# One PSUM bank set from o-projection to down, pools for the next stage's first weights, token sums ahead, and the final norm in halves

## The chip, the cores and the metric

The kernel runs on one core of a Trainium2 chip. The metric is device time in microseconds (us) of one execution. TensorE multiplies matrices into PSUM, eight banks of 512 float32 columns on 128 partitions. VectorE (DVE in the rows), ScalarE (ACT) and GpSimd (POOL) do the element-wise work; SyncE (SP) and ScalarE's queue issue the DMAs. Each engine works through its own queue in order.

## What is computed

The reference is one layer of a hybrid trunk on 2048 frames of a prompt and 8 × 16 frames of running streams, 17 tiles of 128 tokens with 1024 channels. All is float32.

```python
h = rmsnorm(x, norm_mix_pre)
P = h @ w_in
...
o, S_new = gated_delta_rule(q, k, v, g, beta, S0, chunk)
...
mix = jnp.concatenate([o, sc_out.astype(x.dtype)], axis=-1) @ w_o
x = x + rmsnorm(mix, norm_mix_post)

h = rmsnorm(x, norm_ffn_pre)
f = (jax.nn.silu(h @ w_gate) * (h @ w_up)) @ w_down
x = x + rmsnorm(f, norm_ffn_post)
```

`w_gate` and `w_up` are 1024 × 2816, `w_down` is 2816 × 1024.

## The kernel before

A product of two float32 matrices is made of three: each operand is split into a high part, a cast to the multiplier's format, and a low part, the difference. So each weight or token tile needs a cast, on ScalarE, and a subtraction, on VectorE or POOL. Gate/up and down add a seven-product scheme on 2 × 2 blocks in place of eight products, which needs sums of blocks on both sides before the split.

The stages follow each other:

1. In-projection and the gated delta rule, to about 1027 us. The change leaves it alone.
2. o-projection, one `o_tile(t)` (L695) per tile, 17 of them: load `mr` (one buffer) and `xo`, split `mr` in two halves into `mh`, `ml` (L705, L706, three buffers each), 48 matmuls (L711), squares of the sums (L715), norm and addition to `xo` (L720, L721), store to `x2d` (L722), squares of `xo` (L724), scaling of `xo` in place (L727), 8 transposes (L733), scaling by a gain into `ht` (L734), store to `hTd` (L737). After 14 tiles, `ffn_prep(0, ...)` makes the token parts of the first group.
3. Gate/up in three groups of 6, 6 and 5 tiles (`FGROUPS`), 22 blocks f of weights in each. `gate_up` (L903) makes seven products for an f: A11, S3, S1, S2, A12, A22, S4, of 12 matmuls each (L900), 84 in all, with 384 columns (320 in the last group). `gu_weights` loads `rg` and `ru`, makes the sums `sA` to `sD` (L868 to L871) and the seven `fw` pairs (cast L878, subtraction L879), in a ring of 12 pairs. This is done in group 0 only; the pairs with sums are stored in `fsplit` and loaded again in groups 1 and 2. `ffetch` fetches the weights of one f ahead. What comes out of the banks is combined (L918 to L935) into `pt`, seven parts per pair of f (L946 to L956), which goes to `partd` (L958).
4. Between groups, `ffn_prep` makes 28 token parts of the next group: 7 names (B11, T3, T1, T2, B21, T4, B22) for 4 k. Each needs a cast into `xh` (L835) and a subtraction into `xl` (L836); T3, T1, T2, T4 need a block difference first (L821 to L830). The tokens `fh` of the next group are loaded at the start of the group before.
5. Down, five chunks of f (`FCHUNKS`: 4, 4, 4, 4, 6 blocks), in each 8 pairs of token tiles and a single one. `down_pair` (L1051) loads parts `ar`, splits them into `as` (L1011, L1012), and makes seven products (L1028); the last chunk has 63 matmuls per pair. The weight pairs `dw` (L770, L772) live in a ring of 22, 3 of them in an early pool; `prep_step` makes them, some ahead of the next chunk by `spare`. Bank sums are added to `acc` on VectorE (L986).
6. In the last chunk `finish` (L1031) makes the last norm of a tile: load `xr`, square, `rstd` (a step on VectorE, L126, then a power on POOL, L128), multiplication by the gain `gpo` (L1039, on POOL but for the last pair), one operation for scale and addition (L1040), store.

Each stage takes its eight banks from a pool of its own: `psd`, `pst`, `pft` for the o-projection, `psf` for gate/up, `psy` for down. A pool's memory becomes free when the pool before it is closed. Within this, a scheduler that simulates the engines sets the order of the instructions in each queue. `V`, `G`, `A`, `T` are VectorE, POOL, ScalarE and TensorE.

## Time and profile before

| | us |
|---|---|
| runs of the kernel before | 2707.65, 2709.2, 2717.58 |
| median | 2709.2 |
| the profiled execution | 2705.94 |
| its span in the profile | 2704.2 |
| TensorE busy in the span | 2542.4 |
| VectorE, POOL, ScalarE busy | 1687.6, 949.5, 948.0 |

The views are read like this. A row of the timeline gives start, duration, engine, line, operation, output and input, the count, and in brackets how long the engine had stood idle and what ended it. The table of windows gives, for each stretch, the busy time and the count of each engine and the granted clock of TensorE (1.00 is full). L numbers are lines of the kernel before.

### The profile page before, as it was taken

The page shows a single profiled execution, that of the slowest core. Times are in us where ns is not written, and L with a number is a line of the kernel's source. Part 1 is how long each engine was busy: PE and PEld are TensorE (multiplying, and loading weights), DVE is VectorE, ACT ScalarE, POOL GpSimd, SP SyncE. Part 2 cuts the span into 40 slices and gives each one's busy share as a digit, 9 for nine tenths or more (in the row PEclk, how much of TensorE's full clock was granted, in tenths as well). Part 3 has the DMA queues.
Part 4 walks back from the last instruction along what each step waited for, and adds up shares of the span by engine and source line. Part 5 has one row for each costly group of instructions (what it writes and reads, how often), then busy time and mean ns, then how long its engine had stood idle before and what let it go on. Part 6 is the DMA issues. An engine that isn't in the chain of part 4 may idle for free.

```text
span 2704.2 us, 41766 instructions
## 1 busy us (share of the span) xinstructions
PE 2542.4 (94%) x15105; PEld 2359.3 (87%) x15105; DVE 1687.6 (62%) x3341; ACT 948.0 (35%) x2256; POOL 949.5 (35%) x845
## 2 busy tenths in 40 slices
...
PEclk9889999999999999998999989999999989999999
...
GB/s 304 291 306 257 221 212 197 232 195 209 221 215 208 186 237 136 241 167 237 283 259 268 259 223 275 242 257 240 231 310 280 270 176 96 123 121 122 134 203 167
DMA packets 314270, 595.70 MB, mean 220 GB/s; under 512 B 55260, under 2 KB 204704, under 8 KB 292560
## 3 DMA queue, kind: packets, MB, share of 16 engines
...
HBM read 434.04 MB, written 158.90 MB: 219 GB/s over the span
## 4 chain that ended last, share of the span: by engine, by line
PE 39%; DVE 9%; issue 3%; DMA 3%; POOL 2%; ACT 1%; ACTq 1%; SPq 0%; POOLq 0%; DVEq 0%
PE fbank L900 28%; PE ybank L1028 10%; DMA mr<-mixd 1%; DVE xl L836 1%; DMA dr<-in_w_dn 1%; DVE xr L1040 1%; DVE acc L986 1%; POOL as L1012 1%; DMA ru<-in_w_gu 1%; ACTq L958 0%; DVE as L1012 0%; DMA x2d<-xo 0%; POOL dw L772 0%; DVE fw L879 0%; POOL f2r L128 0%
## 5 line engine op out<-in xcount | busy, mean ns | idle before, releaser
L900 PE MATMUL fbank<-xh,fw 128*128 128x384 f32 (+1 forms) x3696 | 906.8, 329 | 17.6 <-ACT m L918 7.4
L134 PE MATMUL dbank<-hi,w 128*128 128x384 f32 (+1 forms) x2688 | 704.0, 341 | 35.3 <-ACT w L293 11.8
L900 PEld LDWEIGHTS fbank<-xh,fw 128*128 128x128 f32 x3696 | 657.4, 190 | 23.8 <-ACT m L918 8.5
L900 PE MATMUL fbank<-xl,fw 128*128 128x384 f32 (+1 forms) x1848 | 605.4, 328 | 2.7 <-DVE xl L836 2.5
L134 PEld LDWEIGHTS dbank<-hi,w 128*128 128x128 f32 x2688 | 493.0, 196 | 48.2 <-ACT w L293 13.6
L1028 PE MATMUL ybank<-dw,as 128*128 128x512 f32 x1980 | 462.5, 395 | 23.7 <-DVE acc L986 10.9
L1028 PEld LDWEIGHTS ybank<-dw,as 128*128 128x128 f32 x1980 | 373.6, 190 | 112.4 <-issue 9.9
L134 PE MATMUL dbank<-lo,w 128*128 128x384 f32 (+1 forms) x1344 | 453.3, 337 | 0.0
L900 PEld LDWEIGHTS fbank<-xl,fw 128*128 128x128 f32 x1848 | 350.0, 190 | 3.2 <-DVE xl L836 2.8
L134 PEld LDWEIGHTS dbank<-lo,w 128*128 128x128 f32 x1344 | 263.9, 196 | 2.2 <-issue 0.2
L879 POOL TENSOR_TENSOR fw<-rg,fw 128x512 fp32r<-128x512 f32 x132 | 184.6, 1399 | 180.6 <-ACT fw L878 180.6
L1012 POOL TENSOR_TENSOR as<-ar,as 128x256 fp32r<-128x256 f32 (+1 forms) x200 | 181.1, 915 | 138.3 <-ACT as L1011 134.6
L986 DVE TENSOR_TENSOR acc<-acc,ybank 128x512 f32<-128x512 f32 x248 | 166.8, 683 | 98.9 <-PE ybank L1028 83.3
L1011 ACT CAST as<-ar 128x256 fp32r<-128x256 f32 (+1 forms) x290 | 118.6, 427 | 196.0 <-PE ybank L1028 135.1
L505 POOL MEMSET AU<- 32x128 f32 x16 | 3.1, 195 | 409.1 <-PE gbank L491 383.7
L878 ACT CAST fw<-rg 128x512 fp32r<-128x512 f32 x132 | 82.4, 624 | 152.2 <-PE fbank L900 137.0
L879 POOL TENSOR_TENSOR fw<-ru,fw 128x512 fp32r<-128x512 f32 x66 | 97.0, 1469 | 108.2 <-ACT fw L878 95.2
L320 DVE SCALAR_TENSOR_TENSOR acc<-R,cw,acc 128x384 f32<-128x384 f32 (+1 forms) x216 | 129.9, 605 | 1.6
L927 DVE TENSOR_TENSOR u<-m,fbank 128x384 f32<-128x384 f32 (+1 forms) x66 | 34.8, 528 | 152.8 <-PE fbank L900 147.8
L928 POOL TENSOR_TENSOR m<-m,m 128x384 f32<-128x384 f32 (+1 forms) x66 | 70.2, 1064 | 148.4 <-ACT m L920 114.2
L932 DVE TENSOR_TENSOR c<-u,fbank 128x384 f32<-128x384 f32 (+1 forms) x66 | 34.9, 528 | 127.7 <-PE fbank L900 127.6
L772 POOL TENSOR_TENSOR dw<-dr,dw 128x512 fp32r<-128x512 f32 x52 | 75.5, 1465 | 29.1 <-ACT dw L770 29.0
...
## 6 DMA issues: line engine op xcount, KB each, us to landing
...
```

The source lines that it names most:

```text
L134: T.matmul(ps, l, r, start=(i == 0), stop=(i == n - 1))
L320: V.scalar_tensor_tensor(acc, raw(d), w[:, d:d + 1], acc, op0=ALU.mult, op1=ALU.add)
L772: e.tensor_tensor(out=w[:, 1], in0=v, in1=w[:, 0].bitcast(F32), op=ALU.subtract)
L878: A.copy(w[:, 0], v)
L879: e.tensor_tensor(out=w[:, 1], in0=v, in1=w[:, 0].bitcast(F32), op=ALU.subtract)
L900: T.matmul(ps, w_[:, c], b_[k][:, :hw], start=(first and k == 0 and ci == 0), stop=(k == KH - 1 and ci == 2), skip_group_check=not first)
L928: G.tensor_tensor(out=s7, in0=s7, in1=s5, op=ALU.add)
L932: V.tensor_add(c21, u2, b3)
L986: V.tensor_add(dst, dst, ps)
L1011: A.copy(a[:, 0, :n], v)
L1012: e.tensor_tensor(out=a[:, 1, :n], in0=v, in1=a[:, 0, :n].bitcast(F32), op=ALU.subtract)
L1028: T.matmul(ps, a[:, x_, q * P:(q + 1) * P], w[:, y_], start=(start and q == 0 and ci == 0), stop=(q == c - 1 and ci == 2), skip_group_chec ...
```

## The change

- **Banks.** `psd`, `pst` and `pft` stay open to the end; `fbank()` goes round their 8 banks in gate/up and down. `psf` and `psy` are gone.
- **o-projection.** `xo` is scaled into a new tile `hx`; `mh` and `ml` have 2 buffers instead of 3; `wor` shares the buffers of `xo`.
- **First weights of gate/up.** A pool `fe` holds `rg`, `ru`, the sums and 3 of the 12 `fw` pairs. It opens ahead of the last three o tiles; `gu_weights` is now a generator, and its first 3 pairs are asked for before the last o tile, the other 4 after it. The subtraction of S4 is on POOL instead of VectorE.
- **Token sums ahead.** `ffn_sums` makes T3 (in 4 buffers) and T1 of the next group inside the group before, all on VectorE. In `ffn_prep` VectorE has 12 of the `xl` subtractions and POOL 16 (14 and 14 before, and POOL had two of the T3).
- **pt and a21** have one buffer instead of two.
- **Down.** 4 instead of 3 weight pairs in the early pool, the ring is 21 instead of 22; the seven parts of the first pair are loaded into a tile `ar0` when the early pool opens, in group 2 at f = 10.
- **Final norm.** Squares, products and additions in halves of 512 columns; the multiplication by `gpo` is one VectorE operation with the scale (none on POOL), the addition another; the halves are stored by ScalarE's and SP's queues. In the last chunk the split of the fourth part is on POOL.

Cut to its core:

```diff
...
-NDR = 3
-NDW = 22
+NDR = 4
+NWE = 3
+NDW = 21
...
-            wr = op.tile([P, D], F32, tag="wor", name="wor", bufs=2)
+            wr = op.tile([P, D], F32, tag="xo", name="wor", bufs=2)
...
-                mh = op.tile([P, KD // 2, P], F32R, tag="mh", name="mh", bufs=3)
-                ml = op.tile([P, KD // 2, P], F32R, tag="ml", name="ml", bufs=3)
+                mh = op.tile([P, KD // 2, P], F32R, tag="mh", name="mh", bufs=2)
+                ml = op.tile([P, KD // 2, P], F32R, tag="ml", name="ml", bufs=2)
...
-            V.tensor_scalar_mul(xt, xt, r)
+            hx = op.tile([P, D], F32, tag="hx", name="hx")
+            V.tensor_scalar_mul(hx, xt, r)
...
+    def fbank():
+        i = nbank[0] % 8
+        nbank[0] += 1
+        pool, tag = (psd, "d") if i < NPD else (pst, "t") if i < NPD + NPT else (pft, "t")
+        return pool.tile([P, 512], F32, tag=tag, name="fbank")
...
-        def ffn_prep(gi, hs, fs):
+        def blocks(gi, hs, k):
+            hw = len(FGROUPS[gi]) * P // 2
+            return hs[k][:, :hw], hs[k][:, hw:2 * hw], hs[KH + k][:, :hw], hs[KH + k][:, hw:2 * hw]
...
+        def ffn_sums(gi, hs, fs):
+            hw = len(FGROUPS[gi]) * P // 2
+            t3 = []
+            for k in range(KH):
+                b11, b12, b21, b22 = blocks(gi, hs, k)
+                t3.append(fs.tile([P, HW], F32, tag="t3", name="ft3", bufs=KH)[:, :hw])
+                V.tensor_sub(t3[k], b22, b12)
+                V.tensor_sub(b12, b12, b11)
...
+        def ffn_prep(gi, hs, t3):
...
-                    e, e2 = (V, G) if k % 2 else (G, V)
-                    if nm == "T3":
-                        v = fs.tile([P, HW], F32, tag="t3", name="ft3")[:, :hw]
-                        e2.tensor_tensor(out=v, in0=b22, in1=b12, op=ALU.subtract)
...
+                    b11, b12, b21, b22 = blocks(gi, hs, k)
+                    if nm == "T2":
+                        V.tensor_sub(b12, b22, b12)
...
+                        V.tensor_sub(b12, b21, b12)
+                    v = {"B11": b11, "B21": b21, "B22": b22, "T3": t3[k]}.get(nm, b12)
...
-                    e.tensor_tensor(out=l[:, :hw], in0=v, in1=h[:, :hw].bitcast(F32), op=ALU.subtract)
+                    (V if k == 3 or (k == 1 and nm not in ("T2", "T4")) else G).tensor_tensor(
+                        out=l[:, :hw], in0=v, in1=h[:, :hw].bitcast(F32), op=ALU.subtract)
...
+            hs = ffn_load(0, fs)
+            hid = ffn_prep(0, hs, ffn_sums(0, hs, fs))
+        fe = ph.enter_context(tc.tile_pool(name="fe", bufs=1, reuse_waits="tile"))
...
-            return fb.tile([P, 2, 512], F32R, tag="w", name="fw", bufs=NWB)
+            pool, b = (fe, NWE) if nw[0] % NWB < NWE else (fb, NWB - NWE)
+            nw[0] += 1
+            return pool.tile([P, 2, 512], F32R, tag="w", name="fw", bufs=b)
...
-            for i, (v, e) in enumerate(((a11, G), (s[2], V), (s[0], G), (s[1], V), (a12, G), (a22, G), (s[3], V))):
+            for i, (v, e) in enumerate(((a11, G), (s[2], V), (s[0], G), (s[1], V), (a12, G), (a22, G), (s[3], G))):
...
-            return out
+                yield w[:, 0], w[:, 1]
...
-        def ffetch():
-            if forder:
+        def ffetch(n=7):
+            if n == 7 and not forder:
...
+            if not fpend or len(fpend[-1][2]) == 7:
...
+            for _ in range(n):
+                fpend[-1][2].append(next(fpend[-1][3]))
...
+        for t in range(O_SPLIT, NT):
+            if t == NT - 1:
+                ffetch(NWE)
+            o_tile(t)
...
+        fb = ph.enter_context(tc.tile_pool(name="fb", bufs=1, reuse_waits="tile"))
...
+        ffetch(7 - NWE)
...
-                pt = fb.tile([P, 7, HW], F32, tag="pt", name="pt", bufs=2)
-                a21 = fb.tile([P, HW], F32, tag="a21", name="a21", bufs=2)
+                pt = fb.tile([P, 7, HW], F32, tag="pt", name="pt")
+                a21 = fb.tile([P, HW], F32, tag="a21", name="a21")
...
-                if gi == len(FGROUPS) - 1 and f >= 10:
-                    if f == 10:
...
-                    elif f >= NF - 2 * NDR and f % 2:
...
+                if gi + 1 < len(FGROUPS):
+                    if f == NF - 6:
+                        t3 = ffn_sums(gi + 1, hs, fd)
+                elif f == 10:
...
+                    dr = late.enter_context(tc.tile_pool(name="dr", bufs=1, reuse_waits="tile", side="right"))
+                    c = len(FCHUNKS[0]) // 2
+                    a = dr.tile([P, 7, c * P], F32, name="ar0")
+                    nc.sync.dma_start(out=a, in_=partd[0][0][0].rearrange("p i q c -> p i (q c)"))
+                    first_parts = [a[:, i] for i in range(7)]
+                    dprep += [down_chunk(ch) for ch in dorder]
+                    prep_step(2)
+                elif 10 < f <= 10 + NDR:
+                    prep_step(1)
...
-        def finish(v, places, final):
+        def finish(v, places):
...
-            A.activation(junk, v, AF.Square, accum_out=ss[:, 0:1])
+            for h in range(2):
+                A.activation(junk, v[:, h], AF.Square, accum_out=ss[:, h:h + 1])
+            V.tensor_add(ss[:, 0:1], ss[:, 0:1], ss[:, 1:2])
...
-            (V if final else G).tensor_tensor(out=v, in0=v, in1=gpo, op=ALU.mult)
-            V.scalar_tensor_tensor(xt, v, r, xt, op0=ALU.mult, op1=ALU.add)
...
-                nc.scalar.dma_start(out=yr[r0:r0 + n], in_=xt[p0:p0 + n])
+            for h in range(2):
+                c = slice(512 * h, 512 * h + 512)
+                V.scalar_tensor_tensor(v[:, h], v[:, h], r, gpo[:, c], op0=ALU.mult, op1=ALU.mult)
+                V.tensor_add(xt[:, c], xt[:, c], v[:, h])
+                for p0, (r0, n) in places:
+                    (nc.sync if h else nc.scalar).dma_start(out=yr[r0:r0 + n, c], in_=xt[p0:p0 + n, c])
...
-            parts = load_parts(src, 0, 4) + load_parts(src, 4, 7)
+            parts = first_parts if (ch, u) == (0, pairs[0]) else load_parts(src, 0, 4) + load_parts(src, 4, 7)
...
-                product(b, ch, split(parts[i], V if i in (0, 3) else G), i, mid)
+                product(b, ch, split(parts[i], V if i in ((0,) if end else (0, 3)) else G), i, mid)
...
```

TensorE's queue at the end of the o-projection before; `xo` is the token tile, `ftbank` takes its transposes, and the last row is the first matmul of gate/up:

```order
L711 MATMUL dbank<-woh_11219,ml 128x512
L711 MATMUL tbank<-woh_11219,ml 128x512
L733 MATMUL ftbank<-cst,xo 128x128 [waits DVE_49,PE_49]
L733 MATMUL ftbank<-cst,xo 128x128 x3
L733 MATMUL ftbank<-cst,xo 128x128 [waits PE_49]
L733 MATMUL ftbank<-cst,xo 128x128 x3
L733 MATMUL ftbank<-cst,xo 128x128 [waits DVE_49,PE_49]
L733 MATMUL ftbank<-cst,xo 128x128 x3
L733 MATMUL ftbank<-cst,xo 128x128 [waits PE_49]
L733 MATMUL ftbank<-cst,xo 128x128 x3
L900 MATMUL fbank<-xh,fw 128x384 [waits Activation_49]
```

The same place in the changed kernel, from the last matmul of the o-projection to the transposes of tile 15, then around those of tile 16:

```order
L713 MATMUL tbank<-woh_11219,ml 128x512
L923 MATMUL fbank<-xh,fw 128x384
L923 MATMUL fbank<-xl,fw 128x384 [waits Pool_49]
L923 MATMUL fbank<-xh,fw 128x384 [waits Pool_49]
...
L923 MATMUL fbank<-xh,fw 128x384 x2
L736 MATMUL ftbank<-cst,hx 128x128 [waits DVE_49,PE_49]
...
L923 MATMUL fbank<-xh,fw 128x384
L736 MATMUL ftbank<-cst,hx 128x128 [waits DVE_49,PE_49]
L736 MATMUL ftbank<-cst,hx 128x128 x3
L736 MATMUL ftbank<-cst,hx 128x128 [waits PE_49]
L736 MATMUL ftbank<-cst,hx 128x128 x3
L923 MATMUL fbank<-xh,fw 128x384 [waits Activation_49]
```

10 matmuls of gate/up now stand ahead of the transposes of tile 15 and 26 more ahead of those of tile 16; the row that waits for ScalarE is the 37th.

ScalarE's queue from the last stores of `pt` into down, before:

```order
L958 DMA partd_4_122<-pt 896x1x128 [waits DMAHW7_49,DVE_49]
L958 DMA partd_4_122<-pt 896x1x128 [waits DMAHW0_49]
L770 CAST dw<-dr 128x512 x4
L1011 CAST as<-ar 128x256 [waits DMAHW1_49]
L1011 CAST as<-ar 128x256 x3
```

and in the changed kernel:

```order
L981 DMA partd_4_122<-pt 896x1x128 [waits DMAHW0_49,DVE_49]
L981 DMA partd_4_122<-pt 896x1x128 [waits DMAHW1_49]
L1035 CAST as<-ar_21032 128x256 x3
L781 CAST dw<-dr 128x512 x2
L1035 CAST as<-ar_21032 128x256
```

The first three token casts have moved ahead of the weight casts, and wait for no load there.

VectorE's queue in the last chunk while a pair's norm is made, before (`acc` of the pair that ends and of the one that runs):

```order
L1012 TENSOR_TENSOR as<-ar,as 128x384 [waits DMAHW6_49,Activation_49]
L1040 SCALAR_TENSOR_TENSOR xr<-acc_0_22823,f2r,xr 128x1024 [waits DMAHW2_49,DMAHW1_49,Pool_49]
L126 TENSOR_SCALAR f2m<-fss_25940 128x1 [waits DVE_49]
L986 TENSOR_TENSOR acc_1_22909<-acc_1_22909,ybank 128x512 [waits DVE_49,PE_49] x2
L986 TENSOR_TENSOR acc_1_22909<-acc_1_22909,ybank 128x512 [waits PE_49]
L1040 SCALAR_TENSOR_TENSOR xr<-acc_0_22823,f2r,xr 128x1024 [waits DMAHW5_49,DMAHW3_49,Pool_49]
```

and in the changed kernel:

```order
L1013 TENSOR_TENSOR acc_0_23087<-acc_0_23087,fbank 128x512 [waits PE_49]
L1066 SCALAR_TENSOR_TENSOR acc_2_23000<-acc_2_23000,f2r,gpo 128x512 [waits Pool_49]
L1066 SCALAR_TENSOR_TENSOR acc_2_23000<-acc_2_23000,f2r,gpo 128x512
L1062 TENSOR_TENSOR fss_26250<-fss_26250 128x1 [waits Activation_49]
L1036 TENSOR_TENSOR as<-ar,as 128x384 [waits DMAHW1_49,Activation_49]
L1067 TENSOR_TENSOR xr<-xr,acc_2_23000 128x512 [waits DMAHW3_49,DMAHW4_49,DMAHW2_49,DVE_49]
L1013 TENSOR_TENSOR acc_0_23087<-acc_0_23087,fbank 128x512 [waits PE_49]
L1067 TENSOR_TENSOR xr<-xr,acc_2_23000 128x512 [waits DVE_49]
L127 TENSOR_SCALAR f2m<-fss_26250 128x1 [waits DVE_49]
```

Two half products and two half additions stand in place of one operation, with an addition to a bank sum between them.

## Rows read from the trace of the kernel before

**Rows 1.** The page: busy time by engine, and TensorE's clock in 40 slices.

```profile
PE 2542.4 (94%) x15105; PEld 2359.3 (87%) x15105; DVE 1687.6 (62%) x3341; ACT 948.0 (35%) x2256; POOL 949.5 (35%) x845
PEclk9889999999999999998999989999999989999999
```

**Rows 2.** Windows: length, busy (count) of PE, PEld, DVE, ACT, POOL, clock, DMA.

```profile
1241.40:1268.40 27.00, 12.86 (x53) 11.46 (x53) 16.05 (x21) 7.62 (x17) 7.94 (x6) 0.62 0.56 181
1290.00:1340.00 50.00, 46.00 (x253) 45.04 (x252) 45.02 (x51) 19.81 (x39) 30.17 (x21) 0.97 0.83 290
1340.00:1580.00 240.00, 239.10 (x1373) 237.45 (x1372) 184.92 (x225) 98.16 (x201) 144.75 (x101) 1.00 0.77 264
1590.00:1620.00 30.00, 22.82 (x102) 21.08 (x101) 24.43 (x27) 9.33 (x21) 17.96 (x15) 0.77 0.53 164
1900.00:1940.00 40.00, 35.21 (x197) 34.32 (x196) 29.62 (x35) 17.51 (x41) 29.44 (x26) 0.92 0.60 192
2220.00:2560.00 340.00, 333.04 (x1446) 270.45 (x1445) 221.14 (x328) 136.72 (x324) 190.18 (x203) 1.00 0.39 124
2500.00:2550.00 50.00, 50.00 (x220) 41.14 (x219) 28.76 (x49) 16.52 (x41) 21.53 (x29) 1.00 0.34 103
2560.00:2690.00 130.00, 121.39 (x518) 97.64 (x517) 104.63 (x125) 44.73 (x90) 100.33 (x69) 0.99 0.55 186
```

**Rows 3.** Timeline of TensorE after the last matmul of the o-projection.

```profile
1244.87 1.94 PE L733 MATMUL ftbank<-cst,xo 128*128 128x128 f32 x8 [3.33 <-DVE xo L727]
1254.80 1.94 PE L733 MATMUL ftbank<-cst,xo 128*128 128x128 f32 x8 [7.98 <-DVE xo L727]
1258.73 0.69 PE L900 MATMUL fbank<-xh,fw 128*128 128x384 f32 x1 [1.99 <-ACT fw L878]
```

**Rows 4.** Timeline of VectorE in the same place.

```profile
1243.98 0.75 DVE L727 TENSOR_SCALAR xo<-xo,oyr 128x1024 f32<-128x1024 f32 x1 [6.05 <-DMA x2d<-xo]
...
1247.46 0.15 DVE L716 TENSOR_TENSOR oss<-oss 128x1 f32<-128x1 f32 x1
...
1250.45 0.68 DVE L721 TENSOR_TENSOR xo<-xo,tbank 128x512 f32<-128x512 f32 x1
...
1253.90 0.75 DVE L727 TENSOR_SCALAR xo<-xo,oyr 128x1024 f32<-128x1024 f32 x1 [1.26 <-DMA x2d<-xo]
```

**Rows 5.** Timeline of ScalarE in the same place.

```profile
1242.14 0.60 ACT L715 ACTIVATE ojunk<-tbank 128x512 bf16<-128x512 f32 x1
...
1257.50 0.52 ACTq L737 DMA_DIRECT2D hTd<-ht  x1
...
1259.63 0.61 ACT L878 CAST fw<-sB 128x512 fp32r<-128x512 f32 x1
```

**Rows 6.** Timelines of ScalarE and TensorE from gate/up to down.

```profile
2208.99 2.17 ACT L770 CAST dw<-dr 128x512 fp32r<-128x512 f32 x4 [3.50 <-issue]
2211.53 2.08 PE L1028 MATMUL ybank<-dw,as 128*128 128x512 f32 x4 [7.06 <-ACT as L1011]
```

**Rows 7.** The tile `mr`: its loads, from issue to landing.

```profile
DMA to landing us min/median/max: 4.9/5.2/6.5
```

**Rows 8.** Timelines of VectorE and POOL at the group change.

```profile
1594.66 1.37 DVE L827 TENSOR_TENSOR fh<-fh 128x384 f32<-128x384 f32 x1
1606.84 0.55 DVE L836 TENSOR_TENSOR xl<-fh,xh 128x384 fp32r<-128x384 f32 x1
1594.28 1.33 POOL L836 TENSOR_TENSOR xl<-ft,xh 128x384 fp32r<-128x384 f32 x1
```

**Rows 9.** The line of the `partd` stores, from issue to landing.

```profile
DMA to landing us min/median/max: 3.3/5.6/11.3
```

**Rows 10.** Timelines of VectorE and POOL in the last chunk.

```profile
2650.22 2.03 DVE L1040 SCALAR_TENSOR_TENSOR xr<-acc,f2r,xr 128x1024 f32<-128x1024 f32 x1 [1.71 <-POOL f2r L128]
2666.66 2.02 DVE L1040 SCALAR_TENSOR_TENSOR xr<-acc,f2r,xr 128x1024 f32<-128x1024 f32 x1 [1.69 <-POOL f2r L128]
2661.79 3.36 POOL L1039 TENSOR_TENSOR acc<-acc,gpo 128x1024 f32<-128x1024 f32 x1
```

80 lines of the change are left out of this document (27 added, 53 removed).

## The prediction

> **What bounds the kernel now.** I read the page first: TensorE is busy 94% of the span and its granted clock is full in nearly all slices [rows 1]. No matmul is removed, so only the stretches where TensorE is off its steady rate can give time. I looked for them in the table of windows, one stretch after the other, and then asked at each gap, in the timelines, which engine ended it. The steady rates come from two windows: 1373 matmuls in 240 us of gate/up are 0.175 us each, 220 in 50 us of down are 0.227 us [rows 2]. A window loses its length minus its count times that rate. Some matmul records may be missing, so a loss is good to about one us. The profiled execution has a span of 2704.2 us and a time of 2705.9; the median of the runs is 2709.2, and I take the gain off the median. After 1241 us the losses are:
>
> - o-projection to gate/up, 1241.4 to 1268.4: the 53 matmuls are 16 transposes and 37 of gate/up. 37 × 0.175 = 6.5, the transposes 2 × 1.94 = 3.9 at the low clock [rows 3]; 27.0 - 10.4 = 17 us lost (A).
> - start of gate/up, 1290 to 1340: 50 - 253 × 0.175 = 5.7 us (B).
> - group 0 to 1: 30 - 102 × 0.175 = 12.2 us (C), of which 7.2 idle; the rest is the clock, 0.77 of full on 22.8 us busy.
> - group 1 to 2: 40 - 35.2 = 4.8 idle, and 0.08 of 35.2 for the clock = 7.6 us (D).
> - gate/up to down: a wait of 7.06 us (E) [rows 6].
> - down to 2560: 340 - 1446 × 0.227 = 11.8 us (F), mostly at chunk boundaries; the last chunk: 130 - 518 × 0.227 = 12.4 us (G). All windows are in [rows 2].
>
> **The change part by part.**
>
> **A: first weights early, rescale into a second tile.** Now VectorE waits 6.05 us for the store of `xo` of tile 15, because L727 scales the tile that is being stored, and tile 16 queues behind it; L727 of tile 16 waits 1.26 more [rows 4]. ScalarE has tile 16's second square done at 1242.14 + 0.60 + its short read = about 1242.9, yet VectorE's L716 runs only at 1247.46, 4.6 us late [rows 4, 5]. With `hx` both waits go, so the `hTd` issue at 1257.50 comes 4.6 + 1.3 = 5.9 earlier, at 1251.6. Behind it ScalarE casts `sB` (0.61; 1259.63 now) and VectorE subtracts, so S2, the fourth product, can begin near 1253. The order of the changed kernel has 36 matmuls, three products, ahead of it, around the last two sets of transposes: 6.3 us of work that needs nothing of tile 16's norm except a free bank for the third product (freed by its L721 additions, now at 1250.45, then 4.6 earlier). Now the first gate/up matmul runs at 1258.73, after two waits, and the 37th ends the window at 1268.4 [rows 2, 3]. 1268.4 - 1253 = 15; I take 14, since the last three casts and subtractions are still made there, with 10 to 16.
>
> **The rest of the o stage.** L727 waits for the store at other tiles too, but TensorE is mostly covered. `hx` gives perhaps 1 us there. Against it stand `mh` and `ml` with two buffers instead of three. The single `mr` buffer is loaded in 5.2 us (6.5 at most) [rows 7]. With two buffers the second half's cast waits for the second half of the tile before, and the chain behind that is cast 0.61 [rows 5], subtraction 0.73 (0.55 × 512/384 from [rows 8], an estimate), load 5.2, cast 0.61 = 7.1 us. Meanwhile TensorE has 48 × 0.227 = 10.9 us of work, so 3.8 us cover it and I cost it at nothing; without the cover every us is paid up to 17 times. Early weight casts and subtractions in the queues of ScalarE and VectorE, and the `rg`/`ru` issues on SP ahead of loads for the last tiles, sit in that cover too. Together +1, from -5 to +4.
>
> **B.** Three weight pairs and the sums of the first two f are ready: some 6 VectorE operations of 0.7 to 1.8 us (0.55 and 1.37 × 512/384) are gone from a stretch where VectorE is busy 45.0 of 50. But the 8 sums of the next group's tokens land in f0 and f1, queued behind loads of `fh` that can only start when the o pools close; behind them wait the `c`, `pt` and weight sums of f0 to f2. The S4 subtraction goes to POOL; in steady group 0 VectorE (185 of 240) and POOL (145 of 240) have room [rows 2], so there it costs nothing. +2, from -4 to +6.
>
> **C and D.** Operations of VectorE between the groups fall from 28 to 20, POOL's stay 16. Eight at 0.55 [rows 8] are 4.4 of 7.2 us idle; the clock's 5 us should shrink with the idle. Lowest: POOL is late anyway and the clock falls as now, +2; highest: all but 1 us, +11. I take +6. D, half of that: +3, 0 to +6. The partd stores stand behind the casts in ScalarE's queue; now their issue holds casts back.
>
> **pt and a21 with one buffer.** The next `pt` must wait for the store's landing, 5.6 us (3.3 to 11.3) [rows 9]. Behind it in VectorE's queue wait the sums for the next weights. The store goes out once the sums behind the products of an odd f are made, the next write is the product of the f after it: one f, 84 × 0.175 = 14.7 us, less some 3 us for those sums. That is 11 or 12 us of cover, and the banks of the next f give most of a second f. Nothing; a landing of over 20 us would use it up, and each of 33 pairs would pay.
>
> **E.** ScalarE now makes four `dw` casts (2.17 us) before the first `as` [rows 6]; in the new order three `as` come first, and the first parts are loaded early. About +2 (1 to 4); the store issues ahead of them remain.
>
> **F.** One weight pair less can be made ahead at each of four boundaries: 0 to 1.8 us each (a cast of 0.54, and a subtraction of 1.33 × 512/384 at most, an estimate). POOL's lighter last chunk can't help here. -2, from -6 to +1.
>
> **G.** The period of a pair is 2666.66 - 2650.22 = 16.4 us; 63 matmuls need 14.3. VectorE waits 1.7 us for POOL's `f2r`, which stands behind a multiplication of 3.36 [rows 10]. That goes. But VectorE gets four products and four additions of 512 columns, at the same estimate of 0.73 each 5.8 us, in place of two of 2.03, less one split (0.55 to 1.4): from +0.4 to +1.2 on 13.2 busy (104.6/130 × 16.4), with more queued ahead of the additions that free the banks. The period lies between 14.4 and 18; 0 is my value, from -10 to +9. The tail: two products and two additions after the last norm against one operation, but half-size stores on two queues: 0 ± 1.5.
>
> Sum: 14 + 1 + 2 + 6 + 3 + 2 - 2 + 0 = **26 us**, 2709.2 - 26 = **2683**. Terms taken as independent leave about ±14 on it.
>
> **The rivals.**
>
> 1. *VectorE and POOL are one resource.* A VectorE subtraction of 0.55 us takes 1.37 while POOL subtracts, and POOL's then takes 1.33: they go in turn, one of each per 1.3 us [rows 8]. So POOL's operation costs VectorE 0.8. Work moved between the two then saves little: B 0, C 2, D 1. In the last chunk six POOL subtractions × 0.8 on 13.9 (13.2 + 0.7, the contention in the 13.2 counted twice, so an upper end) make a period of 18.7, 8 × 2.3 = 18 lost. 14 + 1 + 0 + 2 + 1 + 2 - 2 - 18 = 0: **2709**. Against it: the bank additions have one operand in PSUM, and POOL loses its longest operations. The Trainium skill, "SBUF — State Buffer", section "Who interferes with whom", states this as a rule: a VectorE instruction with two SBUF inputs contends with a GpSimd instruction that reads SBUF, by an exclusive lock. The trace agrees in the alternation just named.
> 2. *The early weights aren't early*: their pool gets its memory late, or the casts stay behind tile 16's norm. Then A gives only the 5.9 us of `hx`: 26 - 8 = 18, **2691**. Against it: the order shows the casts of three weights about five tiles ahead.
> 3. *Slower: two buffers bind the o stage.* If load and casts go beyond the cover of 3.8 us, because the new `rg`/`ru` loads share the DMA engines or early casts hold ScalarE, each tile gets longer. At 3 us beyond it (a landing of 12 instead of 5.2), 17 × 3 = 51 - 26 = 25 us slower: **2734**. It turns the result from 1.6 us per tile on. The largest landing of 6.5 speaks against it.
>
> **How the numbers follow.** Forecast 0.64, rival 1 0.15, rival 2 0.12, rival 3 0.06, other 0.03. About 0.5%, 13.5 us, can be told from no change. Faster by more (under 2695.7): 0.64 × 0.9 + 0.12 × 0.7 + 0.15 × 0.1 = 0.68. Slower by more: rival 3 and the worst of rival 1, 0.08. Same: 0.24. The range: the forecast's bounds go from 2662 to 2697; the upper end goes up to 2707 to hold rival 2 and part of rival 1. Left out are rival 3, half of rival 1 and little of the forecast, under 0.2.
>
> **What would show it.** A: gate/up matmuls start before the last transposes, the fourth product near 1253, and no clock of 0.5 at 1250. C: no idle over 2 us at the group change; if waits on POOL's `xl` appear, rival 1. G: the spacing of the last-chunk norms, 14.4 or above 17. o stage: tile spacing unchanged at about 12 us; waits of TensorE on `mh` mean rival 3. If A gives less than 8 us, or the last chunk costs over 10, the prediction is wrong.

## The result and the profile after

The changed kernel takes 2724.0 us (median of 4 runs, 2721.3 to 2724.6), the kernel before in the same series 2708.4 (4 runs, 2706.5 to 2717.6). The ratio is 1.0049 [1.0025, 1.0073]: 7 to 20 us slower, where 26 us faster was forecast. The profiled execution took 2723.8 us with a span of 2721.7, 17.5 longer than the span before.

The page of the kernel after, busy time by engine and the clock in 40 slices:

```profile
PE 2556.7 (94%) x15105; PEld 2369.8 (87%) x15105; DVE 1682.4 (62%) x3376; ACT 947.5 (35%) x2290; POOL 942.9 (35%) x861
PEclk8889999999999999999999989999899999999999
```

Nothing in the totals answers to a loss of 17 us; against [rows 1] VectorE and POOL have even become a little less busy. So I cut both traces at the same places: the end of the last o matmul, VectorE's sum `u` of the f with a given number (0 to 65 through the three groups), the last matmul of gate/up, the first and last of down. The part of each in us, before, and the difference in the other kernels' profiled executions (+ is longer); for the o stage the matmuls in the segment are counted at 0.2128 us each, so that a shifted marker doesn't count, and the first stage is corrected likewise. In group 0 `u` is such a shifted marker: that of f 6 comes after 587 matmuls of gate/up before and after 557 in the changed kernel, that of f 20 after 1749 and 1733. So f 6 and f 20 stand in the table for the start of gate/up's 588th and 1750th matmul in every kernel; from f 24 on `u` comes after the same count in all:

| segment | before | after | a_s4v | b_s4g | a_sd2 | a_sp | b_pt1 | a_prep | a_mh3n2 | b_fin |
|---|---|---|---|---|---|---|---|---|---|---|
| first stage and o to tile 6 | 1124.4 | +7.3 | +3.7 | +2.9 | +0.7 | +5.9 | -1.7 | -0.9 | -1.2 | +10.8 |
| o stage, tile 6 to the end | 117.1 | +6.3 | +6.4 | +0.8 | +6.2 | +6.7 | +0.5 | +2.5 | +5.2 | +0.6 |
| last o matmul to f 6 (A, B) | 128.8 | -6.4 | -10.7 | +1.4 | -4.0 | -12.2 | -0.5 | -7.9 | -7.0 | +0.5 |
| group 0, f 6 to f 20 | 203.7 | +9.5 | +1.1 | +10.0 | +9.8 | +7.1 | +0.7 | +10.7 | +10.1 | +0.4 |
| group 0 to 1, f 20 to 24 (C) | 68.6 | +3.4 | +2.9 | -0.2 | +4.8 | -3.8 | -0.7 | -0.2 | +5.1 | 0.0 |
| group 1 to 2, f 42 to 48 (D) | 85.7 | +7.0 | +6.9 | -0.1 | +6.6 | +3.3 | +5.9 | +4.2 | +6.5 | -0.1 |
| rest of group 2 | 214.6 | +0.3 | +0.2 | 0.0 | +3.8 | 0.0 | +1.5 | +0.6 | +0.9 | 0.0 |
| gate/up to down (E) | 7.1 | -1.7 | -2.1 | 0.0 | -2.1 | -5.7 | 0.0 | -2.1 | -2.1 | 0.0 |
| down (F, G) | 479.1 | -8.9 | -8.4 | +0.3 | -4.5 | -2.6 | +0.4 | -5.5 | -5.1 | -2.6 |
| tail | 13.5 | +0.8 | +0.9 | -0.1 | +0.9 | +1.1 | -0.1 | +0.8 | +0.8 | +1.3 |

The rest of group 1 is equal in all of them to 0.1 us. The first row is for nearly all of its length work that no kernel here touches, and yet it varies by 12 us from kernel to kernel, as much among the four built on the kernel before (0 to them, -1.7 to +10.8) as among those built on the changed one. Each kernel has one trace, and the times of the kernel before itself go from 2700.4 to 2718.5 us over all series, so this may as well be scatter from execution to execution. A single time therefore says little here, the single edits below were timed once each, and I go by the segments. Without the first row the change costs 17.5 - 7.3 = 10.2 us, which lies inside the interval of the ratio.

TensorE's waits from the last o matmul to the end of gate/up, summed by what ended them (us in total, times, longest; L numbers are from here on lines of the kernel that the rows are from), in the kernel before:

```profile
PE fbank L900 <- ACT m L918: 7.4, 3, 4.6
PE fbank L900 <- ACT m L919: 3.1, 3, 2.1
PE fbank L900 <- DVE xl L836: 2.5, 1, 2.5
PE fbank L900 <- ACT xh L835: 2.4, 2, 1.3
```

and in the kernel after:

```profile
PE fbank L923 <- ACT m L941: 14.6, 10, 5.3
PE fbank L923 <- ACT m L943: 13.6, 8, 4.6
PE fbank L923 <- ACT m L942: 6.2, 4, 4.1
PE fbank L923 <- ACT fw L888: 4.8, 1, 4.8
```

The lines with `m` are ScalarE's copies out of a bank; TensorE waits for these when ScalarE, VectorE and POOL are late. With the third copy (L920, 1.6 us) they come to 12.1 us before and to 34.4 after, while the waits for token parts (`xh`, `xl`) fall from 5.1 to 0.8. The last line is the wait for the fourth product of f0, below.

The windows of the kernel after that answer to [rows 2] (columns as there): from the last o matmul to the 37th of gate/up, 1290 to 1340, and the two group changes:

```profile
1255.09:1270.30 15.21, 8.49 (x53) 7.61 (x52) 6.48 (x14) 3.98 (x11) 2.39 (x3) 0.88 0.60 203
1290.00:1340.00 50.00, 43.68 (x239) 42.71 (x239) 42.05 (x49) 21.70 (x43) 37.98 (x25) 0.97 0.74 260
1610.00:1650.00 40.00, 29.96 (x137) 28.30 (x136) 26.34 (x34) 13.24 (x28) 25.43 (x20) 0.74 0.66 215
1940.00:1980.00 40.00, 30.14 (x163) 29.33 (x163) 25.96 (x31) 14.45 (x33) 26.27 (x24) 0.83 0.70 229
```

The 16 transposes and 37 matmuls that took 27.0 us take 15.2, at a clock of 0.88 in place of 0.62: that part worked. From there to the 588th matmul, however, the kernel after takes 107.2 us where it was 102.0, so B has become worse. Both group changes have, too: 10.0 and 9.9 us idle where it was 7.2 and 4.8, at a clock of 0.74 and 0.83 where it was 0.77 and 0.92.

### The profile page after: what moved, and what is told of

It is laid out like the page before. It is cut to its first block, busy times and chain, and to the rows that moved or that the text cites. A ratio compares the mean times of both kernels' runs of the same rounds, so it can differ in the third digit from the quotient of the medians.

```text
span 2721.7 us, 41986 instructions
## 1 busy us (share of the span) xinstructions
PE 2556.7 (94%) x15105; PEld 2369.8 (87%) x15105; DVE 1682.4 (62%) x3376; ACT 947.5 (35%) x2290; POOL 942.9 (35%) x861
## 4 chain that ended last, share of the span: by engine, by line
PE 65%; DVE 14%; DMA 8%; issue 4%; ACT 4%; POOL 3%; ACTq 1%; SPq 0%; DVEq 0%; POOLq 0%
PE fbank L923 24%; PE dbank L135 19%; PE fbank L1052 10%; PE tbank L713 3%; PE dbank L713 3%; DMA partd<-pt 2%; DMA wr<-in_w_in 1%; POOL fw L889 1%; DVE acc L322 1%; DVE xl L850 1%; DVE acc L1013 1%; ACTq L981 1%; DMA dt<-grow 1%; DMA grow<-rw 1%; DVE xr L1067 1%
## 5 line engine op out<-in xcount | busy, mean ns | idle before, releaser
L923 PE MATMUL fbank<-xh,fw 128*128 128x384 f32 (+1 forms) x3696 | 914.2, 330 | 39.9 <-ACT m L941 14.6
L1052 PE MATMUL fbank<-dw,as 128*128 128x512 f32 x1980 | 461.9, 394 | 13.6 <-ACT as L1035 6.4
L1052 PEld LDWEIGHTS fbank<-dw,as 128*128 128x128 f32 x1980 | 371.8, 189 | 103.6 <-DVE acc L1013 8.4
L1013 DVE TENSOR_TENSOR acc<-acc,fbank 128x512 f32<-128x512 f32 x248 | 166.3, 681 | 96.0 <-PE fbank L1052 82.2
L969 DVE TENSOR_TENSOR pt<-c,m 128x384 f32<-128x384 f32 (+1 forms) x66 | 40.9, 619 | 69.6 <-DMA partd<-pt 47.3
```

The lines of the kernel that those rows point to most:

```text
L923: T.matmul(ps, w_[:, c], b_[k][:, :hw], start=(first and k == 0 and ci == 0), stop=(k == KH - 1 and ci == 2), skip_group_check=not first)
L969: V.tensor_mul(v1, c21, sg0)
L1013: V.tensor_add(dst, dst, ps)
L1052: T.matmul(ps, a[:, x_, q * P:(q + 1) * P], w[:, y_], start=(start and q == 0 and ci == 0), stop=(q == c - 1 and ci == 2), skip_group_chec ...
```

## The experiments

The theory after these traces was that the loss sits in four places with four causes: the subtraction of S4 on POOL (group 0, C), the single `pt` (D), the token sums all on VectorE (o stage, C), and two `mh`/`ml` buffers. The rivals were one common cause, VectorE and POOL taking turns wherever work was moved, and rival 3 of the prediction, the buffers.

**S4's subtraction back on VectorE (a_s4v), and on POOL alone in the kernel before (b_s4g).**

```diff
-            for i, (v, e) in enumerate(((a11, G), (s[2], V), (s[0], G), (s[1], V), (a12, G), (a22, G), (s[3], G))):
+            for i, (v, e) in enumerate(((a11, G), (s[2], V), (s[0], G), (s[1], V), (a12, G), (a22, G), (s[3], V))):
```

> The changed kernel with one edit taken back: the low part of S4 is subtracted on VectorE again. In the trace of the changed kernel group 0 of gate/up runs in pairs of f of 30.9 us instead of 29.3, and VectorE waits up to 4.1 us in front of sD (one buffer) for POOL's subtraction that reads sD, which itself comes behind a cast that ScalarE makes only after the issue of the partd stores. Theory: S4 on POOL is what costs group 0, so pairs go back to 29.3 us, 7 to 11 us are gained there and the time is about 2714. Rival: the single pt buffer costs it; then pairs stay at 30.9 us and the time at 2724.

b_s4g is the opposite edit on the kernel before.

> The kernel before with one edit of the change: S4's low part is subtracted on POOL. Theory (S4 on POOL is a cause by itself, through the stores in ScalarE's queue and through VectorE's turn with POOL): f 6 to f 20 of group 0 gets 8 to 12 us longer than its 203.8 us, the change of groups 1 to 4 us longer, time 2717 to 2725. Rival (it costs only together with the single pt or the early pool of the change): f 6 to 20 within 3 us of before, time 2708 to 2711.

a_s4v: 2707.3 us (before beside it 2710.7). b_s4g: 2721.3 (before 2707.9). Group 0 falls from +9.5 to +1.1 when the subtraction goes back, and gets +10.0 when it alone is moved; A and B, which hold the first f of group 0, gain about 4 more when it goes back. C gets nothing from it alone (-0.2, where 1 to 4 was expected). Over all segments but the first, a_s4v is 2.7 us faster than before, the kernel after 10.2 slower: this one letter is worth more than the whole loss. Waits of TensorE from 1400 to 1580, and the window, for the kernel before:

```profile
PE fbank L900 <- ACT m L919: 0.6, 1, 0.6
1400.00:1580.00 180.00, 179.10 (x1027) 177.52 (x1026) 138.67 (x169) 72.87 (x150) 108.61 (x76) 1.00 0.76 265
```

for the kernel before with S4 on POOL (b_s4g):

```profile
PE fbank L900 <- ACT m L920: 5.0, 6, 1.1
PE fbank L900 <- ACT m L918: 2.1, 6, 0.3
1400.00:1580.00 180.00, 172.90 (x979) 169.06 (x979) 131.08 (x151) 68.90 (x141) 114.70 (x83) 1.00 0.71 249
```

The clock is full in both; TensorE does 48 matmuls less. Per f of 84 matmuls VectorE is busy 138.67/1027 × 84 = 11.34 us before and 131.08/979 × 84 = 11.25 with one subtraction less, POOL 8.88 and 9.84. So the step took 0.09 us off VectorE and put 0.96 on POOL: what VectorE no longer did itself (0.88 us on average), it lost again beside POOL. Its subtraction of `sC` went from 1.32 to 1.55 us on average, the sum `sC` from 1.15 to 1.39. POOL has the time on average (64% busy), but not where it stands. POOL of the kernel after in an odd f, in order of time:

```profile
1436.44 1.29 POOL L889 TENSOR_TENSOR fw<-sD,fw 128x512 fp32r<-128x512 f32 x1 [4.29 <-ACT fw L888]
1437.69 1.01 POOL L951 TENSOR_TENSOR m<-m,m 128x384 f32<-128x384 f32 x1
1438.66 1.74 POOL L889 TENSOR_TENSOR fw<-rg,fw 128x512 fp32r<-128x512 f32 x1
1440.36 1.46 POOL L956 TENSOR_TENSOR m<-m,u 128x384 f32<-128x384 f32 x1
1441.79 1.74 POOL L889 TENSOR_TENSOR fw<-sA,fw 128x512 fp32r<-128x512 f32 x1
```

ScalarE ahead of it, VectorE's sum `sA` behind it, and the wait of TensorE in that f and the next:

```profile
1433.20 2.51 ACTq L981 DMA_DIRECT2D partd<-pt  x3
1435.75 0.62 ACT L888 CAST fw<-sD 128x512 fp32r<-128x512 f32 x1 [4.66 <-issue]
1436.28 0.47 ACT L943 COPY m<-fbank 128x384 f32<-128x384 f32 x1
...
1443.57 1.76 DVE L880 TENSOR_TENSOR sA<-ru 128x512 f32<-128x512 f32 x1 [0.72 <-POOL fw L889]
...
1436.80 0.44 PE L923 MATMUL fbank<-xh,fw 128*128 128x384 f32 x1 [0.84 <-ACT m L943]
1447.84 0.44 PE L923 MATMUL fbank<-xh,fw 128*128 128x384 f32 x1 [0.35 <-ACT m L941]
```

POOL cannot begin until ScalarE has issued three stores of `pt` (2.51 us) and cast `sD`; from there its operations run back to back, and VectorE's `sA` waits for the run's subtraction that reads the only buffer of `sA`, with the sums of `pt`, the combination `c` and, through them, the copy `m` L941 behind it. S4 adds 1.29 us in front of the run. The kernel before had the same run without it, and VectorE already waited for that subtraction. VectorE's waits from 1340 to 1580 in the kernel before, and two rows of its timelines:

```profile
DVE sA L869 <- POOL fw L879: 11.0, 14, 1.7
...
1485.84 1.09 POOL L928 TENSOR_TENSOR m<-m,m 128x384 f32<-128x384 f32 x1 [5.10 <-issue]
...
1491.78 1.76 DVE L869 TENSOR_TENSOR sA<-ru 128x512 f32<-128x512 f32 x1 [0.71 <-POOL fw L879]
```

14 waits in 16 f: in the steady state POOL was on the loop, though it was idle 40% of the time, and only what the loop had to spare hid it from TensorE. The price in the steady state is 1.6 us for a pair of f: 168 matmuls take 30.9 us where they took 29.4. A second buffer of `sA`, which would take this one wait away, wasn't tried.

**Is it the single `sD` buffer? (a_sd2: the kernel after, `sD` with two buffers, 2 early pairs for room.)**

```diff
-NWE = 3
+NWE = 2
...
-                s = [fe.tile([P, 512], F32, tag=nm, name=nm) for nm in ("sA", "sB", "sC", "sD")]
+                s = [fe.tile([P, 512], F32, tag=nm, name=nm, bufs=2 if nm == "sD" else 1) for nm in ("sA", "sB", "sC", "sD")]
```

> The changed kernel with S4 still subtracted on POOL, but sD in two buffers, so that VectorE's next sD does not wait for POOL's subtraction (two early weight pairs instead of three make the room). With S4 on VectorE group 0 kept 29.3 us for a pair of f. Theory: the price of S4 on POOL is this wait for the single sD; then pairs are back at 29.3 to 29.6 us with POOL still doing the subtraction, 8 to 11 us gained in group 0, time about 2712. Rival: POOL itself is late (its queue, or the operations that it makes VectorE wait for); pairs stay at 30.5 us or more, time about 2722.

2728.2 us; group 0 at +9.8 is as in the kernel after, and C at +4.8 no better. VectorE's wait for POOL to read `sD` (39.9 us in 12 waits from 1400 to 1580 in the kernel after) is gone, so it is not what costs; VectorE now waits there for ScalarE's casts (25.3) and for POOL in front of `sA` (14.9).

**Is it the stores in ScalarE's queue? (a_sp: the kernel after, `partd` and `lastd` stored by SP.)**

```diff
-                    nc.scalar.dma_start(out=lastd[ch][:, kk % 2, q, vi * 64:vi * 64 + 64], in_=v[:, hw - 64:hw])
+                    nc.sync.dma_start(out=lastd[ch][:, kk % 2, q, vi * 64:vi * 64 + 64], in_=v[:, hw - 64:hw])
...
-                    nc.scalar.dma_start(out=partd[gi][ch][j, :, :, q, :], in_=pt[:, :, j * P:(j + 1) * P])
+                    nc.sync.dma_start(out=partd[gi][ch][j, :, :, q, :], in_=pt[:, :, j * P:(j + 1) * P])
```

> The changed kernel with one edit: the stores of pt (partd, lastd) are issued from SyncE's queue instead of ScalarE's. In the changed kernel TensorE waits for bank copies on ScalarE (L941 to L943) that stand behind such a store, and the store waits for VectorE's last pt sum; S4 on POOL, the single sD, the single pt and the group changes all seem to reach TensorE by this road. Theory (the road is the store's place in ScalarE's queue): group 0, 11 us over before between f 6 and f 20, falls to under 3; the waits of 3.6 and 4.6 us at the two group changes go; time about 2705. Rival (POOL and VectorE are the limit themselves): group 0 stays 8 or more over, time 2716 or more; SyncE's weight loads, now behind waiting stores, can add waits of their own.

2705.8 us (before 2708.5). Group 0 falls only to +7.1, where under 3 was expected; C falls from +3.4 to -3.8, D from +7.0 to +3.3, and A and B gain 5.8 more. Over all segments but the first this kernel is 6.2 us faster than before: with S4 still on POOL, the stores alone undo the whole loss as well, so the parts of the loss depend on each other. Waits of TensorE from 1400 to 1580 and from 1900 to 2010 in this kernel:

```profile
PE fbank L923 <- ACT m L941: 6.4, 6, 1.8
...
PE fbank L923 <- ACT m L941: 4.3, 1, 4.3
PE fbank L923 <- DMA fw<-fsplit: 3.2, 1, 3.2
```

The waits for `m` L943, the copy behind the stores (5.4 us from 1400 to 1580 in the kernel after), are gone; those for L941, the end of the loop over POOL and VectorE, have grown from 2.1. In group 0, then, the road through ScalarE's stores is about 2 of 9.5 us. The other 7 can't be put on POOL alone: SP's stores now stand ahead of weight loads, and in D TensorE waits for one of these. At the group changes, by contrast, the stores were the larger part.

**One `pt` and one `a21` in the kernel before (b_pt1).**

```diff
-                pt = fb.tile([P, 7, HW], F32, tag="pt", name="pt", bufs=2)
-                a21 = fb.tile([P, HW], F32, tag="a21", name="a21", bufs=2)
+                pt = fb.tile([P, 7, HW], F32, tag="pt", name="pt")
+                a21 = fb.tile([P, HW], F32, tag="a21", name="a21")
```

> The kernel before with one edit of the change: pt and a21 have one buffer. Theory: nothing on TensorE's path, since VectorE's waits for the landing of partd (47 us in 13 places in the changed kernel) lie beside matmuls; group 0 keeps 29.3 us for a pair of f, the group changes move by less than 2 us, the time is 2708 to 2711. Rival: the single buffer costs 1.5 us for each pair of group 0 and some us at each group change, 2720 to 2735.

2712.0 us. Group 0 +0.7 and C -0.7 are nothing, but D gets +5.9, where under 2 was expected, and the rest of group 2 +1.5. Timelines of this kernel at D, VectorE, ScalarE and TensorE:

```profile
1981.86 0.49 DVE L946 TENSOR_TENSOR pt<-c,m 128x320 f32<-128x320 f32 x1 [8.89 <-DMA fw<-fsplit]
...
1982.38 0.33 ACTq L950 DMA_DIRECT2D lastd<-pt  x1
1982.81 0.42 ACT L920 COPY m<-fbank 128x320 f32<-128x320 f32 x1 [8.49 <-DVE pt L946]
...
1983.29 0.42 PE L900 MATMUL fbank<-xh,fw 128*128 128x320 f32 x1 [3.12 <-ACT m L920]
```

VectorE waits 8.9 us to write `pt` anew; the row blames a load of weights, but with two buffers this operation waits for no DMA anywhere in group 2, and with one it does nine times from here on, four of them put down to `partd<-pt`. The stores of the old `pt` had been issued at 1968.91, 12.9 us before the write. The store of `lastd` in ScalarE's queue waits for that `pt`, the copy `m` L920 stands behind it for 8.5 us, and TensorE for 3.1. In group 2, the one with a `lastd`, both stores share ScalarE's queue with every copy out of a bank, so a late `pt` reaches TensorE by two steps.

**Token sums as before (a_prep): the kernel after with the old `ffn_prep`, nothing made ahead.**

```diff
-                    if f == NF - 6:
-                        t3 = ffn_sums(gi + 1, hs, fd)
...
-                hid = ffn_prep(gi, hs, t3)
+                hid = ffn_prep(gi, hs, fd)
...
-            hid = ffn_prep(0, hs, ffn_sums(0, hs, fs))
+            hid = ffn_prep(0, hs, fs)
```

> The changed kernel with the token parts made as before: no sums ahead, two T3 on POOL, the xl subtractions alternating between VectorE and POOL. Theory: the sums and their order cost the o stage its stall at tiles 7 to 9 (9 to 10 us, TensorE waiting for mh and ml whose cast and subtraction stand behind token casts and sums), and the two group changes 5.7 and 7 us, because three of four T2 and T4 subtractions are on POOL: the time falls by 15 to 22, to 2702 to 2709. Rival: two buffers of mh and ml make the o stall, and the issue of the partd stores ahead of the bank copies makes the group changes: all stay within 3 us, time 2720 to 2724.

2708.2 us. The o stage falls from +6.3 to +2.5, C from +3.4 to -0.2, D from +7.0 to +4.2. The sums ahead and the new division of the `xl` subtractions, which this run doesn't part, were meant to help C and D; they cost about 3 us in each and 4 us in the o stage. The timelines of the kernel after show that last one, around tile 8 (ScalarE, VectorE, TensorE):

```profile
1148.05 0.92 ACT L849 CAST xh<-fh 128x384 fp32r<-128x384 f32 x2
1148.87 0.51 ACT L849 CAST xh<-ft 128x384 fp32r<-128x384 f32 x1
1149.29 0.61 ACT L707 CAST mh<-mr 128x512 fp32r<-128x512 f32 x1
...
1149.18 2.63 DVE L833 TENSOR_TENSOR fh<-fh 128x384 f32<-128x384 f32 x2
1151.74 1.35 DVE L832 TENSOR_TENSOR ft<-fh 128x384 f32<-128x384 f32 x1
1155.49 0.67 DVE L708 TENSOR_TENSOR ml<-mr,mh 128x512 fp32r<-128x512 f32 x1
...
1149.95 0.50 PE L713 MATMUL dbank<-woh,mh 128*128 128x512 f32 x1 [1.86 <-ACT mh L707]
1156.21 0.79 PE L713 MATMUL dbank<-woh,ml 128*128 128x512 f32 x1 [4.75 <-DVE ml L708]
```

The cast `mh` stands behind a run of `xh` casts, the subtraction `ml` behind sums and subtractions of group 0's tokens; TensorE waits 6.6 us for the two halves of one tile. All eight sums of group 0 are now on VectorE, within 11 us (1144 to 1155), in the middle of the o stage.

**Three `mh` and `ml` (a_mh3n2): the kernel after with the old buffers, 2 early pairs for room.**

```diff
-NWE = 3
+NWE = 2
...
-                mh = op.tile([P, KD // 2, P], F32R, tag="mh", name="mh", bufs=2)
-                ml = op.tile([P, KD // 2, P], F32R, tag="ml", name="ml", bufs=2)
+                mh = op.tile([P, KD // 2, P], F32R, tag="mh", name="mh", bufs=3)
+                ml = op.tile([P, KD // 2, P], F32R, tag="ml", name="ml", bufs=3)
```

> The changed kernel with three buffers of mh and ml again; to make room for them only two instead of three weight pairs are early. Theory (queue order, not buffers): the stall of 9 to 10 us at tiles 7 to 9 of the o stage stays, time 2722 to 2728. Rival (buffers): the stall is gone, tile spacing 12 us throughout, time about 2715.

2719.5 us. The o stage goes from +6.3 to +5.2 only: rival 3's mechanism is worth about 1 us. Its sign had appeared, since TensorE waits 2.5 us for `mh` and 6.5 for `ml` after 1120 in the kernel after; with three buffers these waits are gone, but one of 5.5 for `hx` comes in their place. A and B lose nothing with two early pairs instead of three.

**The final norm alone (b_fin): the kernel before with `finish` in halves and the fourth split of the last chunk on POOL.**

```diff
-            (V if final else G).tensor_tensor(out=v, in0=v, in1=gpo, op=ALU.mult)
-            V.scalar_tensor_tensor(xt, v, r, xt, op0=ALU.mult, op1=ALU.add)
+            for h in range(2):
+                c = slice(512 * h, 512 * h + 512)
+                V.scalar_tensor_tensor(v[:, h], v[:, h], r, gpo[:, c], op0=ALU.mult, op1=ALU.mult)
+                V.tensor_add(xt[:, c], xt[:, c], v[:, h])
...
-                product(b, ch, split(parts[i], V if i in (0, 3) else G), i, mid)
+                product(b, ch, split(parts[i], V if i in ((0,) if end else (0, 3)) else G), i, mid)
```

> The kernel before with only the final norm of the change: halves on VectorE, no multiplication on POOL, the fourth split of the last chunk on POOL. Down took 479.1 us from first to last matmul before and 470.2 in the changed kernel. Theory: the gain is the last chunk's, the spacing of its pairs falls from 16.4 to about 15.4 us, down takes 471 to 473, time 2701 to 2704. Rival: the larger early pool and the early parts give it at the chunk boundaries; spacing stays at 16.4, down at 479, time 2709.

2716.8 us, of which 10.8 is the untouched first stage, so its total tells nothing. Down is 2.6 shorter, the tail 1.3 longer. By chunks it says more: the last chunk, from its first matmul to its last, took 135.4 us before, 130.9 here and 131.1 in the kernel after, so the norm in halves gives the whole gain there, about 4.4 us, and 3 with the tail. In the total the first chunk hides this: 91.3 us before, 93.4 here, but also 93.0 in b_s4g, whose down is that of the kernel before.

**The good parts together.** Segments as above (+ is longer than before):

| segment | a_s4v_mh3n2_prep | best1 | best1_sp | best3 |
|---|---|---|---|---|
| first stage | +4.4 | +5.9 | +7.7 | +5.1 |
| o stage | +1.5 | -0.7 | +0.2 | +1.3 |
| A, B | -6.1 | -5.8 | -13.1 | -13.3 |
| group 0 | -1.5 | -0.7 | -0.5 | -0.7 |
| C | +0.2 | 0.0 | -2.3 | -2.7 |
| D | +5.2 | -0.1 | +0.2 | +3.3 |
| E | -2.1 | 0.0 | +6.9 | 0.0 |
| down | -8.3 | -5.0 | -5.7 | -4.5 |

The first is a_s4v, a_mh3n2 and a_prep in one kernel: S4 on VectorE, three `mh` and `ml`, 2 early pairs, the old `ffn_prep`.

```diff
-NWE = 3
+NWE = 2
...
-            for i, (v, e) in enumerate(((a11, G), (s[2], V), (s[0], G), (s[1], V), (a12, G), (a22, G), (s[3], G))):
+            for i, (v, e) in enumerate(((a11, G), (s[2], V), (s[0], G), (s[1], V), (a12, G), (a22, G), (s[3], V))):
```

> The changed kernel with three parts taken back: S4 on VectorE, token parts made as before, three buffers of mh and ml (two early weight pairs). What stays is one bank set, the early pool, hx, one pt buffer, the down stage and the final norm of the change. Theory: o stage and start of gate/up 10 to 15 us faster than before, group 0 and its change within 2 us of before, the change from group 1 to 2 still 4 to 6 us slower (single pt), down 5 to 8 us faster: 2690 to 2698. Rival (the parts taken back were not independent causes, the early weights themselves hold the queues): 2703 or more.

2700.7 us, 0.9956 [0.994, 0.9972] of before, 3 us above the range expected. The o stage and the start of gate/up are 4.6 us faster than before, where 10 to 15 was expected: A and B give 6.1 here and 10.7 in a_s4v, and why is open. D still costs 5.2, and that is the single `pt`. best1 gives `pt` and `a21` two buffers again, and pays with the early parts of down:

```diff
-NDR = 4
+NDR = 3
...
-NDW = 21
+NDW = 22
...
-                pt = fb.tile([P, 7, HW], F32, tag="pt", name="pt")
+                pt = fb.tile([P, 7, HW], F32, tag="pt", name="pt", bufs=2)
...
-            parts = first_parts if (ch, u) == (0, pairs[0]) else load_parts(src, 0, 4) + load_parts(src, 4, 7)
+            parts = load_parts(src, 0, 4) + load_parts(src, 4, 7)
```

> The run before it with pt and a21 in two buffers; the room comes from the down stage's early pool (three pairs, no early parts, ring of 22). Theory: the single pt costs 4 to 6 us where group 1 turns into group 2, as it did alone in the kernel before; that goes, E loses up to 2, so 2 to 5 us less than the run before it: 2686 to 2695. Rival: the change from group 1 to 2 is slow through the order of the partd stores in ScalarE's queue whatever the buffers; then it stays and the time is the same or 1 to 3 us more.

2698.2 us, 0.9948 [0.9929, 0.9967], again 3 us above the range: D gives 5.3, down and E are 5.4 longer. Of that only the 2.1 of E is sure, since down varies by 4 us between kernels with the same code for it (after and a_sd2). best1_sp also moves the stores to SP (`lastd` likewise):

```diff
-                    nc.scalar.dma_start(out=partd[gi][ch][j, :, :, q, :], in_=pt[:, :, j * P:(j + 1) * P])
+                    nc.sync.dma_start(out=partd[gi][ch][j, :, :, q, :], in_=pt[:, :, j * P:(j + 1) * P])
```

> The best version so far (S4 on VectorE, token parts as before, three mh and ml, two pt, the early pool, hx, one bank set and the final norm of the change) with the stores of pt issued from SyncE's queue. Theory: the wait of 4.6 us at the change from group 1 to 2 and part of the 12 us at the change from group 0 to 1, which the kernel before has too, go: 2685 to 2693. Rival: VectorE's and POOL's work limits the group changes and SyncE's loads come later: 2697 to 2705.

2695.5 us, 0.9945 [0.9927, 0.9964], 2 us above the range: A and B gain 7.3 more than in best1 and C 2.3, but the first loads of down now stand behind the last stores, and E costs 6.9. best3 keeps the stores of the last group, and `lastd`, on ScalarE:

```diff
-                    nc.scalar.dma_start(out=partd[gi][ch][j, :, :, q, :], in_=pt[:, :, j * P:(j + 1) * P])
+                    (nc.scalar if gi == 2 else nc.sync).dma_start(out=partd[gi][ch][j, :, :, q, :], in_=pt[:, :, j * P:(j + 1) * P])
```

> The best version with the stores of pt on SyncE's queue in groups 0 and 1 only; group 2, from which down starts, has them on ScalarE's again. With all of them on SyncE the start of gate/up was 6 us shorter, and the way from gate/up to down 7 us longer. Theory: the first stays and the second goes: ratio 0.9925, about 2688 to 2693. Rival: the early part is scatter; then the ratio stays at 0.995 and the time at 2696 to 2699.

2692.3 us (6 runs), 0.994 [0.9921, 0.9959]: 16 us less than the kernel before beside it, and 32 less than the changed kernel, which was timed in another series. A, B and C gain the same again; E is back, but D costs 3.3, as it did in a_sp. The intervals of these four overlap, so their order among each other isn't settled by the times; the segments that change are those named.

## Why the prediction was wrong

| term | forecast gain | measured gain |
|---|---|---|
| A and B | 16 | 6.4 |
| rest of the o stage | 1 | -6.3 |
| S4 on POOL, group 0 | 0 | -9.5 |
| C | 6 | -3.4 |
| D | 3 | -7.0 |
| E | 2 | 1.7 |
| F and G | -2 | 8.9 |
| tail and the rest of group 2 | 0 | -1.1 |
| sum (terms rounded) | 26 | -10.2 |

**S4 on POOL is the step that failed most.** "VectorE (185 of 240) and POOL (145 of 240) have room [rows 2], so there it costs nothing" took a mean over a stage for room in a loop. TensorE was 99.5% busy there, so it looked as if only VectorE's sums could matter; but VectorE waited for POOL's queue in nearly every f, and little was spare behind it. Rival 1 had the mechanism (in b_s4g VectorE gains 0.09 us and POOL pays 0.96), but I priced it as savings lost, not as a loss: at 1.6 us per pair it takes 9.5 us from group 0 (10.0 by itself, in b_s4g), and about 4 of what A and B had gained. Its time of 2709 counted down as the place of damage (8 × 2.3 = 18 us); the damage came in group 0, and down became faster. The rule of the Trainium skill named in rival 1, "SBUF — State Buffer", section "Who interferes with whom" (VectorE with two SBUF inputs against GpSimd reading SBUF), fits: with one VectorE subtraction less, VectorE's busy time fell by 0.09 us per f, a small part of the 0.88 us that it took on average from 1400 to 1580 in the trace of before. No run here shows the lock itself.

**C and D: wrong sign.** Counting VectorE's operations, 28 down to 20, was the wrong measure. Between f 20 and f 24 TensorE's waits for `xh` and `xl` did fall, from 4.9 us to 0.8, but those for ScalarE's copies rose from 2.3 to 9.7. In the kernel after VectorE is busy without a break from 1597 to 1627, many of its operations in turns with POOL (rows of 1.3 us for what takes 0.55 alone, [rows 8]), and then:

```profile
1627.35 5.49 ACTq L981 DMA_DIRECT2D partd<-pt  x3
1632.94 0.48 ACT L943 COPY m<-fbank 128x384 f32<-128x384 f32 x1 [5.75 <-issue]
...
1633.47 0.69 PE L923 MATMUL fbank<-xh,fw 128*128 128x384 f32 x1 [3.62 <-ACT m L943]
```

I had written that their issue "holds casts back", and gave it no price: it is 5.5 us here, 4.5 at D. The same three took 4.95 and 2.83 us at these places in the kernel before, but there a cast of token parts stood behind them, not a copy that frees a bank; at C it is this order, more than the length, that is new. C's loss goes with the sums and the division of `xl`: without them it is gone (-0.2, a_prep), and S4 by itself makes none (-0.2, b_s4g). Of D's, 5.9 is the single `pt` (b_pt1); D in a_prep, +4.2, shows that the parts there don't simply add.

**The single `pt`: right for group 0, wrong for D.** The cover of 11 or 12 us holds in group 0, where one `pt` costs about 1 us (+0.7 in b_pt1, +1.1 in a_s4v). At D 12.9 us weren't enough, and I had named VectorE's queue as what stands behind the wait, not ScalarE's, through which it reached TensorE.

**The o stage: the wrong suspect.** I put the danger on two buffers (1 us) and wrote that early sums "sit in that cover". They took about 4 us out of it: cover for a tile of 3.8 us on average is no cover against a run of eight sums and the subtractions behind them.

**A: right in kind, 2 to 3 us too high; B: wrong sign.** Gate/up starts in the same breath as the last o matmul:

```profile
1254.69 0.40 PE L713 MATMUL tbank<-woh,ml 128*128 128x512 f32 x1
1254.93 0.34 PE L923 MATMUL fbank<-xh,fw 128*128 128x384 f32 x1
...
1270.30 0.69 PE L923 MATMUL fbank<-xh,fw 128*128 128x384 f32 x1 [4.84 <-ACT fw L888]
```

From the last o matmul to the 37th of gate/up it was 26.9 us, it is 15.2, so 11.7 of the 14. The rest is a wait that took the place of the one removed. With `hx` the store of `xo` no longer blocks, but `ht` has one buffer (VectorE, then ScalarE, kernel after):

```profile
1267.73 1.29 DVE L737 TENSOR_TENSOR ht<-ftbank,vec 128x512 f32<-128x512 f32 x2 [3.48 <-DMA hTd<-ht]
...
1269.05 0.54 ACTq L740 DMA_DIRECT2D hTd<-ht  x1
1269.63 0.62 ACT L888 CAST fw<-sB 128x512 fp32r<-128x512 f32 x1 [7.24 <-DVE ht L737]
```

Tile 16's `ht` waits for the landing of tile 15's store, issued at 1260.10, and the cast of `sB` stands behind its own store, as the prediction said of the chain. A second `ht` wasn't tried. Rival 2 (early weights not early) fell: they are there. B was to give 2 and took 5.2 (107.2 us to the 588th matmul in place of 102.0); about 4 of it is S4, whose price the term B put at nothing.

**E: right**, 1.7 of 2, by the mechanism given. The store issues that the prediction left ahead of the casts were worth more: with them on SP, E is 1.4 us (a_sp).

**Down: better than forecast.** I gave F -2 and G 0; the two gave 8.9. The last chunk's period went from 16.4 [rows 10] to 15.5:

```profile
2655.97 0.68 DVE L1067 TENSOR_TENSOR xr<-xr,acc 128x512 f32<-128x512 f32 x1
...
2671.48 0.68 DVE L1067 TENSOR_TENSOR xr<-xr,acc 128x512 f32<-128x512 f32 x1
```

The additions of 0.68 leave a gap for the bank additions between them. TensorE's waits for VectorE's `acc` in down fell from 10.9 us to 5.0. So G is the term that was mis-sized: the sum had the waits that go and the operations that come cancel, and the last chunk gave 4.3, the norm alone 4.5 (b_fin). F, the first four chunks, gave 4.6 in the kernel after, but from 2.5 to -2.3 in the five other changed kernels with the same code for down (a_s4v, a_mh3n2, a_prep, a_sd2, a_sp), so what one bank set, the early weights and the early parts do there stays open.
